# A hybrid retention/SSD block on one core: scaling on GpSimd, decay exponentials with a bias, tile places, order at the end

## The chip, the cores and the metric

One program on one core of a Trainium2 chip. The metric is the device time of one execution in microseconds (us); the kernel before took 846.1 us (median of three runs, 846.07 to 846.16).

## The reference

One layer of a streaming encoder over 512 frames, with 16 learned meta tokens ahead of them, width 1024, all in float32:

```python
hn = rmsnorm(h, norm1_w);  proj = hn @ w_in           # 7184 columns: q k v g z x B C dt
y_ret = retention(q, k, v, g)                          # 8 heads of 128, block-causal, decayed state
y_ssd = ssd(z, conv(x B C), dt)                        # 16 heads of 64 in 4 groups, state 128
#   lmat = exp(a_cs[l] - a_cs[s]) for l >= s;  y = (C B^T * lmat) @ (x dt) + C @ state + x * d_skip
#   y = y * silu(z);  y = y * rsqrt(mean(y*y) over the group's 256) * norm_w
h = h + concat(y_ret, y_ssd) @ w_out
h = h + relu(rmsnorm(h, norm2_w) @ w_ff1)**2 @ w_ff2
return rmsnorm(h, final_norm_w)                        # meta rows dropped
```

## The kernel before

Every large product is made of three TensorE passes over operands that are split in a high part and a low rest (high x high, high x low, low x high). The split is done on the fly for every weight tile: ACT copies the raw tile into the high half of a tile `wh`, DVE subtracts to get the low half (`split`, L163 to L165). Raw weights come by DMA into four buffers `wr`, split ones live in four buffers `wh`.

The program runs through these stages: the SSD projections, group by group (`ssd_proj`, four groups g: B, C, two halves of x, then z), with the scan of the group before (`ssd_core`) woven into them; the retention heads (q, k, v, g) with their cores; the output product; the first FFN product in Strassen-like sub-products (`product`); the second FFN product; and the last norm. A framework scheduler then sets the order of every engine's instructions by its own estimates of when operands are ready. Each engine works its stream strictly in that order, so an instruction that waits holds all behind it.

**Places.** A split tile starts at a multiple of 256 bytes, and the class `cls` of a unit shifts it by 64 bytes times the class (`wh_tile`). The other operand is the split normalised input `hnh`/`hnl`, read from column 0 (meta tokens and 256 frames: products of 272 columns), from column 16 (all frames), or from column 272 (products of 256 columns), which lie 0, 64 and 64 bytes past a multiple of 256. For q, k, v, g, x, B, C the weights are stationary and the input moves; for z it is the other way round. "Distance" below is stationary start minus moving start, modulo 256 bytes, in steps of 64. Before, the products of 256 columns have distance 0 for x, 1 for B, C and k, 2 for v; z has 1, 0 and 3 in the groups 1, 2 and 3.

**The scan of a group.** `lt` (four heads, 128 x 512 each) is loaded by DMA from a DRAM copy of the running sums (`acsd`, L504). `decay` makes the decay matrix of each head: for each of four chunks DVE adds a per-partition value and takes the minimum with 0 (L509), then ACT takes one Exp of the whole head (L510); later DVE multiplies by the masked C B^T (L574). Products `yo` and `yd` give y, DVE gates it with silu(z) (L593), ACT takes squares with sums (L596), GpSimd makes (mean + eps)^-0.5 (L600, L601), DVE scales the four chunks of y (L603), TensorE transposes y (`ytp`, L610) and ACT writes it out (L611).

**ACT's tables.** Exp and Silu need different tables; a load (ACT_TABLE_LOAD) stands wherever the stream goes from one to the other.

**The end.** For each of four row blocks b, `fin_b` adds the product to the residual on DVE (L1065), squares on ACT (L1067), (sum)^-0.5 on GpSimd (L1073, L1074), and `scale_b` (L1083 to L1086) scales one half on DVE and one on ACT, with a DMA each. `scale_b(b - 1)` is written behind the add of block b.

Of the kernel before, what the change touches and what calls it, by code (L numbers as in the profile page):

```python
# [37 lines left out]
C_Q, C_K, C_V, C_G, C_Z, C_X, C_B, C_C, C_DT = 0, 1024, 2048, 3072, 4096, 5120, 6144, 6656, 7168  # L38
# [37 lines left out]
def kernel(ctx, tc, x, meta, xtr, wzd, nfw, w_in, w_out, w1, w2, hrows, pcols, crope, cmask, cpack, cident, out, gpow):  # L76
    nc = tc.nc
    ACT, DVE, POOL, PE = nc.scalar, nc.vector, nc.gpsimd, nc.tensor
# [9 lines left out]
    whl = ctx.enter_context(tc.tile_pool(name="whl", bufs=4))  # L88
# [7 lines left out]
    xt = [perm.tile([P, D], F32, name=f"xt{b}") for b in range(NB)]  # L96
# [17 lines left out]
    tna = sp.tile([P, NCH, SH], F32, name="tna")  # L114
# [78 lines left out]
    def u_cols(w, c0, c1, cls=(2, 2)):  # L193

        def ld(c, j):
            return (lambda r: r[:, j * 1024:(j + 1) * 1024].rearrange("p (k c) -> p k c", c=P),
                    w[:, c:c + P].rearrange("(k p) c -> p k c", p=P))
        if c1 == c0 + P:
            loads = [(lambda r: r.rearrange("p (k c) -> p k c", c=2 * P),
                      w[:, c0:c0 + 2 * P].rearrange("(k p) c -> p k c", p=P))]  # L200
            views = lambda r, j: r.rearrange("p (k c) -> p k c", c=2 * P)[:, :, j * P:(j + 1) * P]
        else:
            loads = [ld(c0, 0), ld(c1, 1)]
            views = lambda r, j: r[:, j * 1024:(j + 1) * 1024].rearrange("p (k c) -> p k c", c=P)
        return Unit(loads, views, P, cls)

    def u_z(w, c0, cls):

        loads = [(lambda r: r.rearrange("p (k c) -> p k c", c=256),
                  w[:, c0:c0 + 256].rearrange("(k p) c -> p k c", p=P))]  # L210
        return Unit(loads, lambda r, j: r[:, j * 1024:(j + 1) * 1024].rearrange("p (k c) -> p k c", c=256), 256, (cls, cls))

    class UnitZ0(Unit):

# [25 lines left out]
    def add(key, u):  # L240
        U[key] = u
        order.append(u)

    add(("z", 0), UnitZ0())
    for g in range(SG):
        add(("bc", g), u_cols(w_in, C_B + P * g, C_C + P * g))
        add(("x", g), u_cols(w_in, C_X + 256 * g, C_X + 256 * g + P, (1, 1)))
        if g:
            add(("z", g), u_z(w_in, C_Z + 256 * g, (g - 1) % 3))
    for h in range(RH):  # L250
        add(("qk", h), u_cols(w_in, C_Q + P * h, C_K + P * h, (1, 2)))
# [245 lines left out]
    def ssd_core(g, r):  # L497
        bf, cf, xf = r["bf"], r["cf"], (r["x0"], r["x1"])
        hs = slice(4 * g, 4 * g + 4)

        pl = [sw.tile([P, T], F32, tag="lt", name="lt", bufs=4) for _ in range(4)]
# [3 lines left out]
        def decay(h):  # L505
            hh = 4 * g + h
            for c in range(NB):
                v = pl[h][:, c * P:(c + 1) * P]
                DVE.tensor_scalar(v, v, tna[:, c + 1, hh:hh + 1], 0.0, op0=ALU.add, op1=ALU.min)  # L509
            ACT.activation(pl[h], pl[h], AF.Exp)  # L510


        xdt = sw.tile([P, NB, 256], F32, tag="xdt", name="xdt", bufs=1)
# [56 lines left out]
        cbm = sw.tile([P, T], F32, tag="cbm", name="cbm", bufs=1)  # L570
        DVE.tensor_tensor(cbm.rearrange("p (c l) -> p c l", l=P), ps.rearrange("p (c l) -> p c l", l=P),
                          tri.unsqueeze(1).broadcast_to([P, NB, P]), op=ALU.mult)
        for h in range(4):
            DVE.tensor_tensor(pl[h], cbm, pl[h], op=ALU.mult)  # L574
        yield
        y = sw.tile([P, NB, 256], F32, tag="y", name="y", bufs=1)
        ss = small.tile([P, NB], F32, tag="ss4", name="ss4")
        for c2 in range(2):
            po = psum(pm, "yo")
            for cc in range(2):  # L580
                c = 2 * c2 + cc
# [5 lines left out]
            for cc in range(2):  # L587
                c = 2 * c2 + cc
# [5 lines left out]
            for cc in range(2):  # L594
                c = 2 * c2 + cc
# [3 lines left out]
        rs = small.tile([P, NB], F32, tag="rs4", name="rs4")  # L599
        POOL.tensor_scalar(rs, ss, 1.0 / 256, EPS, op0=ALU.mult, op1=ALU.add)  # L600
        POOL.tensor_tensor(rs, rs, powc[:, :NB], op=ALU.pow)  # L601
        for c in range(NB):
            DVE.tensor_scalar(y[:, c, :], y[:, c, :], rs[:, c:c + 1], None, op0=ALU.mult)  # L603
        yield
        if g < SG - 1:
            yield
# [30 lines left out]
    for g in range(SG):  # L637
        r = {} if g else r0
# [106 lines left out]
    for h in range(RH):  # L745
        r = {}
# [106 lines left out]
    def split_hs(q, pool, src):
        t = HS.get(q)
        if t is None:
            t = HS[q] = pool.tile([P, 2, 4, 256], F32R, name=f"hs{q}")
        split(t[:, 0].rearrange("p k n -> p (k n)"), t[:, 1].rearrange("p k n -> p (k n)"), src)

    def tok_gen(b):

        for _ in range(LAG):
            yield
        h = b // 2
        for j in range(2):
            ps = psum(pm, "tp")
            for k in range(4):
                PE.transpose(ps[:, k * P:(k + 1) * P], xt[b][:, (4 * j + k) * P:(4 * j + k + 1) * P], ident)
            dst = R[j][h].rearrange("p (k n) -> p k n", n=256)[:, :, (b % 2) * P:(b % 2 + 1) * P]
            for k in range(4):
                ACT.activation(dst[:, k, :], ps[:, k * P:(k + 1) * P], AF.Copy, scale=pc[:, PC_N2 + 4 * j + k:PC_N2 + 4 * j + k + 1])  # L870
            if b == 1:
                split_hs(1 + j, None, R[j][0])
            yield
        if b < 3:
            return
        sub = lambda o, x, y: DVE.tensor_tensor(o, x, y, op=ALU.subtract)
        t2 = FP["a"][:, 14:16, :].rearrange("p a b -> p (a b)")
        sub(R[0][0], R[0][1], R[0][0])
        sub(t2, R[1][1], R[0][0])
        while "t" not in FP:  # L880
            yield
        split_hs(6, FP["t"], t2)
        yield
        split_hs(5, FP["t"], R[0][0])
        sub(R[0][1], R[1][1], R[0][1])
        yield
        split_hs(7, FP["t"], R[0][1])
        yield
        sub(R[1][0], R[1][0], t2)
        split_hs(4, FP["t"], R[1][0])  # L890
        yield
        split_hs(3, FP["t"], R[1][1])
# [13 lines left out]
    loads = [0, 2, 4, 1, 6, 7] + list(range(8, 2 * NG))  # L906
# [31 lines left out]
    for g in range(NG):  # L938
        p = at[(6, g)]
# [3 lines left out]
    def w1_prep(n, pool=None):  # L943
        if n >= len(seq) or n in wsp:
            return
        q, g = seq[n]
        src = {1: lambda: quarter(g, 0, 0), 2: lambda: quarter(g, 0, 1), 3: lambda: quarter(g, 0, 1), 4: lambda: quarter(g, 1, 1),
               5: lambda: s1s[g], 6: lambda: quarter(g, 0, 0), 7: lambda: quarter(g, 1, 0)}[q]()
        t = wh_tile(pool or whl, 1)
        split(t[:, 0, :], t[:, 1, :], src)  # L950
        wsp[n] = t.rearrange("p y (k c) -> p y k c", c=256)
        if q == 3:
            done.add(2 * g)
        if all(at[(i, g)] in wsp for i in (4, 7)):
            done.add(2 * g + 1)
        next_loads()
# [25 lines left out]
    def product(n):  # L982
# [95 lines left out]
    def scale_b(b):  # L1078
        o = out[b * P:(b + 1) * P, :]
        w = 256 if b == NB - 1 else 512  # L1080
        for c in range(0, 512, w):
            l, r = slice(c, c + w), slice(512 + c, 512 + c + w)
            DVE.scalar_tensor_tensor(yo[b][:, r], xt[b][:, r], rss[b], nwb[:, r], op0=ALU.mult, op1=ALU.mult)  # L1083
            nc.sync.dma_start(out=o[:, r], in_=yo[b][:, r])
            ACT.activation(yo[b][:, l], yo[b][:, l], AF.Copy, scale=rss[b])
            nc.scalar.dma_start(out=o[:, l], in_=yo[b][:, l])  # L1086

    FP["s"].release()
# [10 lines left out]
    nwb = fin.tile([P, D], F32, name="nwb")  # L1099
# [53 lines left out]
```

## Time and profile before

| | |
|---|---|
| median of three runs | 846.1 us |
| the profiled execution | 847.2 us, of it the span 845.4 us |
| PE (matmul) busy | 832.1 us, 98% of the span |
| DVE, ACT, POOL busy | 556.5, 411.2, 29.8 us |
| ACT table loads | 24, 1.28 us each |
| mean granted TensorE clock | 0.998 of 2.4 GHz |

A busy PE in this profile is an engine with matmuls in flight. They overlap: one of 256 columns is listed with about 0.28 us, but the next one starts 0.11 to 0.12 us after it. So rates are read from starts, not from durations.

### The profile page before, as it was taken

What the parts mean: (1) busy time and instruction counts of PE and PEld (TensorE: products, weight loads), DVE (VectorE), ACT (ScalarE), POOL (GpSimd) and SP (SyncE); (2) the same over time, 40 slices, a digit from 0 to 9 for tenths busy, and PEclk for the clock granted to TensorE, in tenths of its full rate; (3) what the DMA queues carried; (4) which work ended last, traced back from release to release, by engine and by line L of the source; (5) the groups of instructions that cost most, each with busy time, mean ns of one, the idle gap of its engine ahead of it and who ended that gap; (6) DMA issues with size and microseconds to landing.
All of it is one profiled execution on the core that took longest, in us unless ns stands there. A gap on an engine that the chain in (4) does not pass through costs nothing.

```text
span 845.4 us, 13366 instructions
## 1 busy us (share of the span) xinstructions
PE 832.1 (98%) x5556; PEld 759.2 (90%) x5556; DVE 556.5 (66%) x874; ACT 411.2 (49%) x693; POOL 29.8 (4%) x62
## 2 busy tenths in 40 slices
PE   8999999999999999999999999999999999999996
PEld 7999999999889999999888889999999888888884
DVE  6788997968745554556365539988887554474442
ACT  7755737272422233232453548577667643354432
POOL 1000000010000000000000000000000000010001
PEclk9999999999999999999999999999999999999999
DMA  9751333332331313131213213333334523332002
GB/s 316 252 178 50 100 101 100 95 106 76 101 100 50 100 51 100 51 101 50 100 53 102 96 50 100 101 100 101 100 101 137 188 100 99 100 100 100 0 1 100
DMA packets 85373, 84.70 MB, mean 100 GB/s; under 512 B 2464, under 2 KB 67744, under 8 KB 85312
## 3 DMA queue, kind: packets, MB, share of 16 engines
q1 hardware_dynamic: 84016, 81.68, 30.7%
q10 hardware_dynamic: 1296, 2.16, 0.7%
q8 instruction: 43, 0.70, 0.3%
q14 instruction: 18, 0.15, 0.1%
HBM read 81.71 MB, written 2.13 MB: 99 GB/s over the span
## 4 chain that ended last, share of the span: by engine, by line
PE 90%; DVE 3%; ACT 3%; DMA 2%; issue 2%; POOL 0%; POOLq 0%; ACTq 0%; SPq 0%
PE acc L781 10%; PE acc L782 10%; PE acc L780 10%; PE fb L998 7%; PE fd L998 5%; PE fa L998 4%; PE pz L473 3%; PE pj L344 3%; PE pj L342 3%; PE pj L343 3%; PE pv L344 2%; PE pv L343 2%; PE pv L342 2%; PE pk L342 2%; PE pk L344 2%; PE pk L343 2%
## 5 line engine op out<-in xcount | busy, mean ns | idle before, releaser
L164 ACT ACTIVATE wh<-wr 128x1024 fp32r<-128x1024 f32 x146 | 153.8, 1057 | 207.2 <-issue 81.6
L165 DVE TENSOR_TENSOR wh<-wr,wh 128x1024 fp32r<-128x1024 f32 x146 | 177.8, 1219 | 107.4 <-ACT wh L164 107.2
L781 PE MATMUL acc<-wh,mh 128*128 128x512 f32 x370 | 144.1, 390 | 0.5 <-DVE mh L165 0.5
L780 PE MATMUL acc<-wh,mh 128*128 128x512 f32 x370 | 144.2, 391 | 0.0
L782 PE MATMUL acc<-wh,mh 128*128 128x512 f32 x370 | 144.1, 389 | 0.0
L781 PEld LDWEIGHTS acc<-wh,mh 128*128 128x128 f32 x370 | 69.5, 188 | 15.0 <-DVE mh L165 0.9
L782 PEld LDWEIGHTS acc<-wh,mh 128*128 128x128 f32 x370 | 69.5, 188 | 14.6
L780 PEld LDWEIGHTS acc<-wh,mh 128*128 128x128 f32 x370 | 69.4, 188 | 14.0
L342 PE MATMUL pj<-hnh,wh 128*128 128x256 f32 (+2 forms) x256 | 73.7, 288 | 0.0
L343 PE MATMUL pj<-hnl,wh 128*128 128x256 f32 (+2 forms) x256 | 73.2, 286 | 0.0
L344 PE MATMUL pj<-hnh,wh 128*128 128x256 f32 (+2 forms) x256 | 72.5, 283 | 0.0
L998 PE MATMUL fb<-hs,wh 128*128 128x256 f32 x576 | 68.4, 277 | 0.4 <-DVE wh L165 0.4
L998 PEld LDWEIGHTS fb<-hs,wh 128*128 128x128 f32 x576 | 66.8, 188 | 0.7 <-DVE wh L165 0.6
L343 PEld LDWEIGHTS pj<-hnl,wh 128*128 128x128 f32 x256 | 48.5, 189 | 0.1
L342 PEld LDWEIGHTS pj<-hnh,wh 128*128 128x128 f32 x256 | 48.4, 189 | 0.0
L344 PEld LDWEIGHTS pj<-hnh,wh 128*128 128x128 f32 x256 | 48.4, 189 | 0.0
L998 PE MATMUL fa<-hs,wh 128*128 128x256 f32 x384 | 46.3, 277 | 0.3 <-ACT a_lo L1003 0.3
L998 PE MATMUL fd<-hs,wh 128*128 128x256 f32 x384 | 45.2, 277 | 0.0
L998 PEld LDWEIGHTS fa<-hs,wh 128*128 128x128 f32 x384 | 44.7, 188 | 0.5 <-ACT a_lo L1003 0.5
L998 PEld LDWEIGHTS fd<-hs,wh 128*128 128x128 f32 x384 | 44.5, 188 | 0.1
L164 ACT ACTIVATE mh<-a_lo 128x512 fp32r<-128x512 f32 x48 | 29.3, 621 | 19.2 <-PE acc L782 17.1
L165 DVE TENSOR_TENSOR mh<-a_lo,mh 128x512 fp32r<-128x512 f32 x48 | 32.5, 687 | 7.7 <-ACT mh L164 7.6
(270 smaller groups left out, 1646.6 us busy)
## 6 DMA issues: line engine op xcount, KB each, us to landing
wr<-in_w_ff_dram SPq DMA_DIRECT2D x30, 1024.0 KB, 5.3
wr<-in_w_in_dram SPq DMA_DIRECT2D x40, 512.0 KB, 4.8
wr<-in_w_out_dram SPq DMA_DIRECT2D x8, 1024.0 KB, 5.0
wr<-in_w_in_dram SPq DMA_DIRECT2D x7, 1024.0 KB, 8.1
lt<-acsd SPq DMA_DIRECT2D x16, 256.0 KB, 4.2
xt<-in_x_dram SPq DMA_DIRECT2D x4, 512.0 KB, 6.8
a_lo<-in_w_ff_dram SPq DMA_DIRECT2D x2, 1024.0 KB, 6.4
wzr<-in_wzd_dram ACTq DMA_DIRECT2D x4, 272.0 KB, 6.1
```

Source lines behind the costliest of these rows:

```text
L164: ACT.activation(dst_h, src, AF.Copy)
L165: DVE.tensor_tensor(dst_l, src, dst_h.bitcast(F32), op=ALU.subtract)
L342: PE.matmul(ps[:, :n], lhsT=wh[:, k, :], rhs=hnh[:, k, t0:t0 + n], start=(k == 0), stop=False)
L343: PE.matmul(ps[:, :n], lhsT=wh[:, k, :], rhs=hnl[:, k, t0:t0 + n], start=False, stop=False)
L344: PE.matmul(ps[:, :n], lhsT=wl[:, k, :], rhs=hnh[:, k, t0:t0 + n], start=False, stop=(k == KT - 1))
L473: PE.matmul(o, lhsT=a[:, k, tk], rhs=zp[k // 4][y][:, k % 4, :], start=(i == 0), stop=(i == len(seq) - 1))
L780: PE.matmul(acc[b], lhsT=s[:, 0, tk], rhs=wh[:, kk, :], start=(k == 0), stop=False)
L781: PE.matmul(acc[b], lhsT=s[:, 1, tk], rhs=wh[:, kk, :], start=False, stop=False)
L782: PE.matmul(acc[b], lhsT=s[:, 0, tk], rhs=wl[:, kk, :], start=False, stop=(k == nk - 1))
L998: PE.matmul(o, lhsT=w[:, y, k, cs], rhs=h[:, z, k, :], start=(q in (1, 6, 5) and t == 0 and k == 0 and i == 0), stop=(k == 3 and i == 2), ...
```

## The change

- `decay`: the 64 DVE instructions (add, minimum) and 16 Exps of 128 x 512 become 64 Exps of 128 x 128 on ACT that take the added value as their bias; the minimum moves into the multiply by C B^T, now min with 1 and multiply (a scalar_tensor_tensor on DVE, 16 of them).
- The four scalings of y of each group go from DVE to GpSimd, behind its power.
- Classes: x from 1 to 2, z from 0, 1, 2 to 0, v from 3 to 2. The distances of all products of 256 columns become 1; those of 272 columns become 2 for x (were 1) and 2 for v (were 3). In the first FFN product `wh` goes from class 1 to 2 and the input tiles `hs` move by 64 bytes as well, so that the distance stays 1; their pool is now filled in one place.
- In `scale_b` the DVE and the ACT scaling are pinned behind what is written before them on their engine.

```diff
-    def u_z(w, c0, cls):
+    def u_z(w, c0):
...
-        return Unit(loads, lambda r, j: r[:, j * 1024:(j + 1) * 1024].rearrange("p (k c) -> p k c", c=256), 256, (cls, cls))
+        return Unit(loads, lambda r, j: r[:, j * 1024:(j + 1) * 1024].rearrange("p (k c) -> p k c", c=256), 256)
...
-        add(("x", g), u_cols(w_in, C_X + 256 * g, C_X + 256 * g + P, (1, 1)))
+        add(("x", g), u_cols(w_in, C_X + 256 * g, C_X + 256 * g + P))
...
-            add(("z", g), u_z(w_in, C_Z + 256 * g, (g - 1) % 3))
+            add(("z", g), u_z(w_in, C_Z + 256 * g))
...
-        add(("vg", h), u_cols(w_in, C_V + P * h, C_G + P * h, (3, 1)))
+        add(("vg", h), u_cols(w_in, C_V + P * h, C_G + P * h, (2, 1)))
...
-                DVE.tensor_scalar(v, v, tna[:, c + 1, hh:hh + 1], 0.0, op0=ALU.add, op1=ALU.min)
-            ACT.activation(pl[h], pl[h], AF.Exp)
+                ACT.activation(v, v, AF.Exp, bias=tna[:, c + 1, hh:hh + 1])
...
-            DVE.tensor_tensor(pl[h], cbm, pl[h], op=ALU.mult)
+            DVE.scalar_tensor_tensor(pl[h], pl[h], 1.0, cbm, op0=ALU.min, op1=ALU.mult)
...
-            DVE.tensor_scalar(y[:, c, :], y[:, c, :], rs[:, c:c + 1], None, op0=ALU.mult)
+            POOL.tensor_scalar(y[:, c, :], y[:, c, :], rs[:, c:c + 1], None, op0=ALU.mult)
...
+    hs12.tile([P, 16], F32, name="pad3")
     HS = {q: hs12.tile([P, 2, 4, 256], F32R, name=f"hs{q}") for q in (1, 2)}
...
-        t = wh_tile(pool or whl, 1)
+        t = wh_tile(pool or whl, 2)
...
+                FP["t"].tile([P, 16], F32, name="pad5")
+                HS.update({q: FP["t"].tile([P, 2, 4, 256], F32R, name=f"hs{q}") for q in (6, 5, 7, 4, 3)})
...
-            DVE.scalar_tensor_tensor(yo[b][:, r], xt[b][:, r], rss[b], nwb[:, r], op0=ALU.mult, op1=ALU.mult)
+            tc.keep_in_program_order(
+                DVE.scalar_tensor_tensor(yo[b][:, r], xt[b][:, r], rss[b], nwb[:, r], op0=ALU.mult, op1=ALU.mult))
             nc.sync.dma_start(out=o[:, r], in_=yo[b][:, r])
-            ACT.activation(yo[b][:, l], yo[b][:, l], AF.Copy, scale=rss[b])
+            tc.keep_in_program_order(ACT.activation(yo[b][:, l], yo[b][:, l], AF.Copy, scale=rss[b]))
```

What this does to the streams is shown at three places. The first is ACT while the scan of group 0 starts (`xf` is the second half of x after its convolution, which TensorE transposes next; `btm` a transposed piece of B, `hq` the first state). Before:

```order
L527 ACTIVATE bt_685<-btp_692 128x384
L164 ACTIVATE wh_907<-wr_822 128x1024
L427 ACT_TABLE_LOAD
L427 ACTIVATE xf_672<-acc_667,pc_84 128x528
L510 ACT_TABLE_LOAD
L510 ACTIVATE lt_674<-lt_674 128x512
L523 ACTIVATE btm_109<-mtp_686 16x128
L510 ACTIVATE lt_675<-lt_675 128x512
L164 ACTIVATE wh_998<-wr_996 128x1024
L559 ACTIVATE hq_803<-st0_797 128x256
```

The same place now:

```order
L526 ACTIVATE bt_685<-btp_692 128x384
L164 ACTIVATE wh_903<-wr_818 128x1024
L509 ACTIVATE lt_674<-lt_674,tna_101 128x128 x2
L427 ACT_TABLE_LOAD
L427 ACTIVATE xf_672<-acc_667,pc_84 128x528
L509 ACT_TABLE_LOAD
L509 ACTIVATE lt_674<-lt_674,tna_101 128x128
L522 ACTIVATE btm_109<-mtp_686 16x128
L509 ACTIVATE lt_674<-lt_674,tna_101 128x128
L509 ACTIVATE lt_675<-lt_675,tna_101 128x128 x4
L509 ACTIVATE lt_676<-lt_676,tna_101 128x128 x4
L509 ACTIVATE lt_677<-lt_677,tna_101 128x128 x4
```

Two Exps of the first head stand ahead of the Silu of `xf`; twelve more and one of the first head stand between `btm` and `hq`.

The second place is the second half of group 1's scan, where y is squared (`xdd`), on ACT; `lt_1701` or `lt_1693` is the first head of group 2. Before:

```order
L427 ACTIVATE cf_1399<-acc_1394,pc_84 128x512
L596 ACTIVATE xdd_1197,ss4_1402<-y_1401 128x256 x2
L164 ACTIVATE wh_1582<-wr_1579 128x1024
L596 ACTIVATE xdd_1197,ss4_1402<-y_1401 128x256 x2
L427 ACTIVATE xf_1483<-acc_1478,pc_84 128x528
```

Now:

```order
L595 ACTIVATE xdd_1193,ss4_1394<-y_1393 128x256 x2
L427 ACTIVATE cf_1391<-acc_1386,pc_84 128x512
L164 ACTIVATE wh_1574<-wr_1571 128x1024
L509 ACT_TABLE_LOAD
L509 ACTIVATE lt_1693<-lt_1693,tna_101 128x128
L427 ACT_TABLE_LOAD
L427 ACTIVATE xf_1475<-acc_1470,pc_84 128x528
L595 ACTIVATE xdd_1193,ss4_1394<-y_1393 128x256 x2
```

The second pair of squares now stands behind an Exp of the next group, two table loads and a Silu. On DVE at the same place, from the gating of y on, before:

```order
L593 TENSOR_TENSOR y_1401<-y_1401,zs_1135 128x512
L425 SCALAR_TENSOR_TENSOR acc_1478<-pre_1424,pc_84,acc_1478 128x528
L404 MEMSET pre_1515 128x3
L407 TENSOR_TENSOR pre_1515<-pj_1517,rsr_113 128x272
L165 TENSOR_TENSOR wh_1576<-wr_1510,wh_1576 128x1024
L603 TENSOR_SCALAR y_1401<-y_1401,rs4_1503 128x256 x4
```

Now:

```order
L592 TENSOR_TENSOR y_1393<-y_1393,zs_1131 128x512
L404 MEMSET pre_1507 128x3
L407 TENSOR_TENSOR pre_1507<-pj_1509,rsr_113 128x272
L165 TENSOR_TENSOR wh_1568<-wr_1502,wh_1568 128x1024
L407 TENSOR_TENSOR pre_1507<-pj_1535,rsr_113 128x256
L165 TENSOR_TENSOR wh_1574<-wr_1571,wh_1574 128x1024
L423 TENSOR_SCALAR acc_1561<-pre_1507,pc_84 128x528
L404 MEMSET pre_1735 128x3
L425 SCALAR_TENSOR_TENSOR acc_1561<-pre_1507,pc_84,acc_1561 128x528 x2
L165 TENSOR_TENSOR wh_1732<-wr_1571,wh_1732 128x1024
L425 SCALAR_TENSOR_TENSOR acc_1561<-pre_1507,pc_84,acc_1561 128x528
```

DVE no longer stops for the scaling of y; it runs on through splits and convolution adds while GpSimd scales.

The third place is the end of DVE's stream. Before:

```order
L1065 SCALAR_TENSOR_TENSOR xt0_78<-acc_7408,rs20_4693,xt0_78 128x512
L1083 SCALAR_TENSOR_TENSOR yo0_6894<-xt0_78,rss0_6902,nwb_6885 128x512
L1065 SCALAR_TENSOR_TENSOR xt1_79<-acc_7409,rs21_4694,xt1_79 128x512
L1083 SCALAR_TENSOR_TENSOR yo1_6895<-xt1_79,rss1_6903,nwb_6885 128x512
L1065 SCALAR_TENSOR_TENSOR xt2_80<-acc_7410,rs22_4695,xt2_80 128x512
L1083 SCALAR_TENSOR_TENSOR yo2_6896<-xt2_80,rss2_6904,nwb_6885 128x512
L1065 SCALAR_TENSOR_TENSOR xt3_81<-acc_7411,rs23_4696,xt3_81 128x256 x2
```

Now:

```order
L1067 SCALAR_TENSOR_TENSOR xt0_78<-acc_7396,rs20_4679,xt0_78 128x512
L1067 SCALAR_TENSOR_TENSOR xt1_79<-acc_7397,rs21_4680,xt1_79 128x512
L1086 SCALAR_TENSOR_TENSOR yo0_6882<-xt0_78,rss0_6890,nwb_6873 128x512
L1067 SCALAR_TENSOR_TENSOR xt2_80<-acc_7398,rs22_4681,xt2_80 128x512
L1086 SCALAR_TENSOR_TENSOR yo1_6883<-xt1_79,rss1_6891,nwb_6873 128x512
L1067 SCALAR_TENSOR_TENSOR xt3_81<-acc_7399,rs23_4682,xt3_81 128x256 x2
L1086 SCALAR_TENSOR_TENSOR yo2_6884<-xt2_80,rss2_6892,nwb_6873 128x512
```

The add of each block now stands ahead of the scaling of the block before. ACT's squares and scalings change places in the same way, and its last two scalings alternate with their two DMA issues, where both scalings stood first before.

## Rows read from the trace of the kernel before

**Rows 1.** Page, busy time of the engines (share of the span) xinstructions.
```profile
PE 832.1 (98%) x5556; PEld 759.2 (90%) x5556; DVE 556.5 (66%) x874; ACT 411.2 (49%) x693; POOL 29.8 (4%) x62
```
**Rows 2.** Timeline of PE: start us, us, engine, line, output<-inputs; products for x and z.
```profile
121.14 0.37 PE L342 MATMUL pj<-hnh,wh 128*128 128x272 f32 x1
...
124.19 0.28 PE L342 MATMUL pj<-hnh,wh 128*128 128x256 f32 x1
...
127.06 0.28 PE L473 MATMUL pz<-wh,hnh 128*128 128x256 f32 x1
...
129.94 0.71 PE L610 MATMUL ytp<-idt,y 128*128 128x128 f32 x5
...
172.67 0.28 PE L473 MATMUL pz<-wh,hnh 128*128 128x256 f32 x1
...
175.50 0.71 PE L610 MATMUL ytp<-idt,y 128*128 128x128 f32 x5
```
**Rows 3.** Timeline of PE, one head's products for k and v.
```profile
225.01 0.37 PE L342 MATMUL pk<-hnh,wh 128*128 128x272 f32 x1
...
228.13 0.28 PE L342 MATMUL pk<-hnh,wh 128*128 128x256 f32 x1
...
230.87 0.38 PE L711 MATMUL kv<-mk 128*128 128x128 f32 x2
...
235.69 0.28 PE L342 MATMUL pv<-hnh,wh 128*128 128x256 f32 x1
...
238.57 0.38 PE L727 MATMUL o<-vt,pt 128*128 128x128 f32 x2
```
**Rows 4.** Timeline of ACT at group 0's scan; [idle before <- what ended it].
```profile
52.09 0.74 ACT L427 ACTIVATE xf<-acc,pc 128x528 f32<-128x528 f32 x1 [2.06 <-DVE acc L425]
53.91 1.28 ACT L510 ACT_TABLE_LOAD   x1 [1.08 <-DMA lt<-acsd]
```
**Rows 5.** Timeline of PE at the same place.
```profile
54.62 0.27 PE L519 MATMUL mtp<-idt,xf 128*16 128x128 f32 x1
...
57.42 0.67 PE L553 MATMUL st<-xmw,btm 128*128 128x256 f32 x2 [0.69 <-ACT btm L523]
```
**Rows 6.** Groups by line and form, ACT: xcount | busy us, mean ns | idle before.
```profile
L510 ACT ACT_TABLE_LOAD x9 | 11.5, 1283 | 1.2 <-DMA lt<-acsd 1.1
...
L708 ACT ACTIVATE vt<-vtp,rsc 128x128 f32<-128x128 f32 x32 | 9.0, 369 | 0.0
```
**Rows 7.** Tile lt, 108 to 125 us: loads for group 2, time to landing.
```profile
L503 SPq DMA_DIRECT2D lt<-acsd x4: 338/382/386, 120.7 to 122.1; - x4
...
DMA to landing us min/median/max: 3.2/3.5/4.2
```
**Rows 8.** Timeline of PE at group 0's transposes of y.
```profile
84.68 1.13 PE L610 MATMUL ytp<-idt,y 128*128 128x128 f32 x8 [0.55 <-DVE y L603]
```
**Rows 9.** Timeline of ACT, the squares of group 1's second half.
```profile
123.92 0.42 ACT L596 ACTIVATE xdd<-y 128x256 f32<-128x256 f32 x1 [4.04 <-DVE y L593]
```
**Rows 10.** Timeline of POOL, groups 0 and 1.
```profile
82.84 0.20 POOL L600 TENSOR_SCALAR rs<-ss 128x4 f32<-128x4 f32 x1 [57.53 <-ACT xdd L596]
...
124.92 1.20 POOL L600 TENSOR_SCALAR rs<-ss 128x4 f32<-128x4 f32 x1 [40.78 <-ACT xdd L596]
126.20 1.01 POOL L601 TENSOR_TENSOR rs<-rs,powc 128x4 f32<-128x4 f32 x1
```
**Rows 11.** Timeline of DVE, around the second of these.
```profile
124.85 1.22 DVE L165 TENSOR_TENSOR wh<-wr,wh 128x1024 fp32r<-128x1024 f32 x1
```
**Rows 12.** Timeline of DVE at the end.
```profile
837.87 0.75 DVE L1083 SCALAR_TENSOR_TENSOR yo<-xt,rss,nwb 128x512 f32<-128x512 f32 x1 [1.69 <-POOL rss L1074]
838.54 0.87 DVE L1065 SCALAR_TENSOR_TENSOR xt<-acc,rs,xt 128x256 f32<-128x256 f32 x2
```
**Rows 13.** Timeline of PE and of ACT's queue at the end.
```profile
834.37 2.88 PE L807 MATMUL acc<-wh,mh 128*128 128x512 f32 x12
...
841.49 0.84 ACTq L1086 DMA_DIRECT2D out_dram<-yo  x2
```

More of the change, by code (lines that the diff above doesn't have):

```diff
@@ L845 @@
     wx = tc.alloc_tile_pool(name="wx", bufs=3, side="right", reuse_waits="tile")
+    hs12.tile([P, 16], F32, name="pad3")
     HS = {q: hs12.tile([P, 2, 4, 256], F32R, name=f"hs{q}") for q in (1, 2)}
+    hs12.tile([P, 48], F32, name="pad4")
     a_hi = ar.tile([P, 8, T], F32, name="a_hi")
@@ L851, with split_hs @@
     FP = {}
[L853 to L856, printed above, removed]
+    def split_hs(q, src):
+        t = HS[q]
         split(t[:, 0].rearrange("p k n -> p (k n)"), t[:, 1].rearrange("p k n -> p (k n)"), src)
@@ L871, in tok_gen @@
             if b == 1:
-                split_hs(1 + j, None, R[j][0])
+                split_hs(1 + j, R[j][0])
             yield
@@ L881, in tok_gen @@
             yield
-        split_hs(6, FP["t"], t2)
+        split_hs(6, t2)
         yield
-        split_hs(5, FP["t"], R[0][0])
+        split_hs(5, R[0][0])
         sub(R[0][1], R[1][1], R[0][1])
         yield
-        split_hs(7, FP["t"], R[0][1])
+        split_hs(7, R[0][1])
         yield
         sub(R[1][0], R[1][0], t2)
-        split_hs(4, FP["t"], R[1][0])
+        split_hs(4, R[1][0])
         yield
-        split_hs(3, FP["t"], R[1][1])
+        split_hs(3, R[1][1])
     def fin1(b, acc):
@@ L1039, in first_products @@
                 FP["t"] = tc.alloc_tile_pool(name="hst", bufs=1, side="right", reuse_waits="tile")
+                FP["t"].tile([P, 16], F32, name="pad5")
+                HS.update({q: FP["t"].tile([P, 2, 4, 256], F32R, name=f"hs{q}") for q in (6, 5, 7, 4, 3)})
+                FP["t"].tile([P, 48], F32, name="pad6")
             if n == at[(6, 0)]:
```

## The prediction, made before the changed kernel was run

> **What bounds the kernel now.** I read the busy times first: PE has matmuls in flight for 98% of the span, DVE is busy for 66% and ACT for 49% [rows 1]. So only two things move the end: the pace of PE's own products, and the few places where PE waits. I then read PE's timeline, from starts and not from durations. Twenty-four products of 256 columns for k take 230.87 - 228.13 = 2.74 us, for v 238.57 - 235.69 = 2.88 [rows 3]; for x 127.06 - 124.19 = 2.87, for z 2.88 in group 2 and 2.83 in group 3 [rows 2]. Same shape, same number, other distance of the two tiles. Last came the waits of PE and what ended them: 0.55 us at group 0's transposes of y, ended by DVE's scaling [rows 8], and 0.69 at `st`, ended by ACT's copy of `btm` [rows 5]. The profiled execution took 847.17 us, 845.4 of it the span, about 1.1 above the median. I work out differences against it and take them off or add them to the median, 846.1.
>
> **The places.** Distance 1 is the fastest for 256 columns: 2.74 us for 24, against 2.87 at 0 (x), 2.88 at 2 (v), 2.88 at 0 (z, group 2) and 2.83 at 3 (z, group 3) [rows 2, 3]. All of these go to 1. By blocks of 24: v has eight heads, 8 x 0.14 = 1.12; x two halves in four groups, 8 x 0.13 = 1.04; z four blocks in group 2, 4 x 0.14 = 0.56, and four in group 3, 4 x 0.09 = 0.36. Against it stand the 272-column products of x, which go from distance 1 (124.19 - 121.14 = 3.05) to 2; the k products at another distance than 1 show 228.13 - 225.01 = 3.12 [rows 2, 3], so 8 x 0.07 = 0.56 is lost. For v's 272 columns (3 to 2) no row gives both distances; I take nothing, with the same 0.56 either way as bounds. The first FFN product moves both tiles by 64 bytes and keeps its distance: nothing. Sum -1.12 - 1.04 - 0.56 - 0.36 + 0.56 = **-2.5 us**. These products stand on the bound engine, so the whole of it counts where no wait eats it.
>
> **The end.** The last product ends at 834.37 + 2.88 = 837.25 [rows 13], but the last add starts at 838.54, behind the scaling of block 2 that waited for GpSimd until 837.87 [rows 12]. With the add first, up to 838.54 - 837.29 = 1.25 goes. But ACT now has the scaling of block 2 and a DMA issue behind the squares of block 3, and each scaling of block 3 alternates with its issue, where the two issues stood last together (841.49 and half of 0.84 later [rows 13]). So the late thing next is ACT's last issue. Bounds -1.25 and 0; I take **-0.6**, halfway.
>
> **The exponentials off the path.** ACT gets 64 Exps of 128 x 128. The trace has none; the nearest row is a scaled ACTIVATE of that shape, 369 ns each and 9.0 us for 32, so 0.28 a piece when they overlap [rows 6]. Sixty-four are 18 us, less the 16 large ones. The streams hold 38 table loads where there were 24: 14 x 1.283 = 18.0 us more [rows 6]. DVE loses 64 instructions. ACT was half idle, so all of this is worth nothing by itself: PE's products hide it. It matters only where something PE needs soon stands behind it, which is at group 0's start and before the transposes of y.
>
> The rows have the next ACTIVATE right behind a load: one load and its Exp stand 1.28 apart. The Trainium skill (ScalarE: Activation LUTs, the measured figure under the section on what ACT_TABLE_LOAD costs) adds a drain of about 1380 ns to every switch. By that rule the squares of groups 1 and 2, each with one exposed load ahead, would come about 1.4 later each, and my sum would rise by an estimated 2.8; I follow the rows.
>
> **Group 0's start.** Two Exps now stand ahead of the Silu of `xf`. They need `lt`, and `lt` landed when ACT's wait of 1.08 ended, at 53.91 [rows 4]. Then 0.65 for two Exps, 1.28 for the table, 0.74 for the Silu: 53.9 + 0.65 + 1.28 + 0.74 = 56.6. PE wants `xf` at 54.62 [rows 5]: a wait of 2.0. The wait of 0.69 for `btm` falls away, and DVE, which was also behind here, has less to do; PE may be level again by the first `yd`. Bounds 0.3 and 1.3 (2.0 - 0.7); I take **+0.5**, nearer to the low end because the products after it are waiting for DVE anyway.
>
> **The scaling of y on GpSimd.** This is the large term. I walk each group from Y, the start of PE's next projection right behind the last `yd` (121.14 in group 1 [rows 2]). The loads of the next group's `lt` go out at 120.7 = Y - 0.44 and take 3.2 to 4.2, median 3.5 [rows 7], so they land at Y + 3.1. Now Exps stand ahead of the second pair of squares, and a waiting Exp holds the squares, the Silus and the split copies behind it on ACT.
>
> Group 1: Exp 0.37, table 1.28, Silu 0.74 and two squares of 0.42 [rows 4, 6, 9] give Y + 3.1 + 0.37 + 1.28 + 0.74 + 0.84 = Y + 6.35, where the first of these squares started at 123.92 = Y + 2.78 before [rows 9]. GpSimd's power takes at least 0.20 + 1.01 and some 0.2 of gaps [rows 10]: Y + 7.75. PE is at the transposes at Y + 8.8 (129.94 before [rows 2]). So there is 1.05 for four scalings, of which DVE did one in about 0.28 of its 1.14 in all.
>
> What one scaling costs on GpSimd is the unknown. The same small instruction took 0.20 us when DVE stood idle and 1.20 when it started beside DVE's split [rows 10]; it ended at 126.12, the split at 124.85 + 1.22 = 126.07 [rows 11]. So a GpSimd instruction is held until DVE's instruction with two inputs from SBUF is over. DVE's stream now runs such instructions without a stop while GpSimd scales, since the scaling no longer stands in it. Bounds for one scaling: 0.2 and 1.2. I take 0.8: some 0.3 of its own and half a split's wait.
>
> - Group 1: four at 0.8 are 3.2, so Y + 10.95 against Y + 8.8: wait 2.2.
> - Group 2: two more Exps (0.55) ahead of the squares, Y + 11.5 against Y + 8.7: wait 2.8.
> - Group 0: PE comes early, at Y + 6.2, since only 4 products of z stand ahead (24 x 0.127 + 24 x 0.114 + 4 x 0.114). Six Exps (1.7) and two squares: Y + 5.65; power, Y + 7.1; it needs two pieces soon, 1.6: wait 2.5.
> - Group 3: no Exps follow and DVE has little to do; 0.3.
>
> Sum 7.8, less the old wait of 0.55 [rows 8]: **+7.25**, with +2.2 if a scaling takes 0.3, and some +11 if each takes 1.2.
>
> **Total:** -2.5 - 0.6 + 0.5 + 7.25 = +4.65, so 846.1 + 4.65 = **850.8 us**.
>
> **Rivals.**
>
> 1. *GpSimd scales undisturbed, 0.3 a piece.* Waits 1.4 (group 0), 0.2, 0.9 and 0.2, less 0.55: +2.2, and -2.5 - 0.6 + 0.5 + 2.2 = -0.4: **845.7**. For it: 0.20 us beside an idle DVE [rows 10]. Against it: rows 11, and that the two engines meet in every group. This is also what the Trainium skill says where it compares engines (GPSIMD Engine Reference, on engine selection): elementwise work with one input is roughly at line rate there. Yet its specifications table on the same page names contention with DVE instructions of two SBUF inputs, and with that the trace agrees (1.20 against 0.20).
> 2. *The waits vanish (the other side: faster).* If the squares of group 0 end by Y + 4.2 rather than Y + 5.65 and those of group 2 a microsecond sooner, the scaled y is there when PE comes. That takes loads that land after 3.2 [rows 7], Exps at 0.2 and GpSimd at 0.2 a piece. Then only the places, the end and the old wait count, and group 0's start is level: -2.5 - 0.6 - 0.55 = -3.65: **842.5**. Against it: six Exps of 0.28 behind a landing at Y + 3.1 cannot be over by Y + 4.2 unless the loads are issued earlier.
> 3. *Each scaling waits out a whole split, 1.2 a piece.* +1.6 in groups 1 and 2 and +0.8 in group 0 on top of the forecast: 850.8 + 4.0 = **854.8**. For it: the one overlap that I can read ended exactly with the split. Against it: many of DVE's instructions there are shorter than a split.
>
> **How the numbers follow.** Forecast 0.50, rival 1 0.28, rival 2 0.12, rival 3 0.10. About 0.2%, 1.7 us, is what a measurement can tell from no change: 844.4 to 847.8. Faster: all of rival 2 and a third of rival 1 (the tail's 0.6 more, group 0's start at its low end), 0.22. Same: the rest of rival 1 and 0.05 of the forecast's low end (a scaling at 0.5), 0.23. Slower: 0.55. The range goes from 843.2, short of rival 2, to 855.5, past rival 3's value; the forecast's own range is 848 to 853.5.
>
> **What would show it.** Right: PE shows waits of 2 to 3 us at `ytp` in groups 0, 1 and 2, ended by POOL's y; single scalings on POOL near 0.8, their ends on the ends of DVE's splits and convolution adds; 24 products of 256 columns in 2.74 everywhere; a wait of about 2 at `mtp` for `xf` near 54.6; the last add starting near the end of the last product. Wrong: scalings of 0.3 and PE's waits at `ytp` under 1.5 (rival 1); squares that end well before Y + 5 (rival 2); 256-column products of x, v or z still at 2.87 (the places do not do it); or an end that comes no earlier against the last product.

## The result and the profile after

The changed kernel took 868.9 us (median of 4 runs, 867.45 to 869.64) against 846.1 (846.00 to 846.16): ratio 1.026, interval 1.024 to 1.028. It is slower, as forecast, but by 22.8 us where I had forecast 4.7, and the time lies far outside my range. The profiled execution took 867.45 us, 865.7 of it the span, 20.3 more than before. (Before, the profiled execution lay 1.1 above its median, now it lies 1.4 below, so the traces show 20.3 of the 22.8.)

I first lined the two timelines up by the starts of the same products on PE:

| product on PE | before | after | after - before |
|---|---|---|---|
| first `yo`, group 0 | 63.55 | 63.62 | +0.07 |
| first `yo`, group 1 | 110.07 | 115.84 | +5.77 |
| first `yo` of the second half, group 2 | 164.19 | 174.67 | +10.48 |
| the same, group 3 | 209.48 | 225.77 | +16.29 |
| first `o`, head 0 | 238.57 | 260.80 | +22.23 |
| first output product | 412.05 | 433.30 | +21.25 |
| last twelve products | 834.37 | 855.82 | +21.45 |
| end of the span | 845.4 | 865.7 | +20.3 |

So 4.7 to 5.9 us are lost in each of four stretches, which hold the transposes of y of groups 0, 1, 2 and 3. After them the heads give back 1.0 and the end 1.15. PE's busy time is hardly longer than before [rows 1]; the page's line of busy times:

```profile
PE 837.2 (97%) x5556; PEld 763.1 (88%) x5556; DVE 541.3 (63%) x794; ACT 439.9 (51%) x755; POOL 49.3 (6%) x78
```

The waits of PE (line, what it waited for: us in total, times, longest) name the place:

```profile
PE ytp L609 <- POOL y L602: 15.8, 15, 3.4
PE mtp L518 <- ACT xf L427: 1.3, 1, 1.3
```

The first was 0.55, once, for DVE [rows 8]. The timeline of PE shows it from the side of the transposes, in groups 0 and 2:

```profile
84.53 0.44 PE L609 MATMUL ytp<-idt,y 128*128 128x128 f32 x2 [3.45 <-POOL y L602]
86.21 0.47 PE L609 MATMUL ytp<-idt,y 128*128 128x128 f32 x1 [1.25 <-POOL y L602]
...
188.57 0.48 PE L609 MATMUL ytp<-idt,y 128*128 128x128 f32 x1 [2.50 <-POOL y L602]
189.47 0.48 PE L609 MATMUL ytp<-idt,y 128*128 128x128 f32 x1 [0.42 <-POOL y L602]
190.37 0.48 PE L609 MATMUL ytp<-idt,y 128*128 128x128 f32 x1 [0.42 <-POOL y L602]
```

In group 2 a piece arrives every 0.90 us. POOL's timeline has four scalings, one behind the other, in all four groups. They take 1.05 to 1.66 us on the mean of a group; taken one by one they run from 0.92 to 2.46:

```profile
83.47 6.63 POOL L602 TENSOR_SCALAR y<-y,rs 128x256 f32<-128x256 f32 x4
...
135.83 5.16 POOL L602 TENSOR_SCALAR y<-y,rs 128x256 f32<-128x256 f32 x4
...
187.00 4.21 POOL L602 TENSOR_SCALAR y<-y,rs 128x256 f32<-128x256 f32 x4
...
233.68 4.48 POOL L602 TENSOR_SCALAR y<-y,rs 128x256 f32<-128x256 f32 x4
```

What I had not looked for at all stands in the table by stretches (start:end, length, PE busy and count, granted TensorE clock, DMA share, GB/s):

```profile
80.00:104.00 24.00, 18.50 (x141) 0.93 0.29 89
130.00:150.00 20.00, 16.17 (x123) 0.91 0.44 129
180.00:200.00 20.00, 16.23 (x116) 0.83 0.54 159
226.00:246.00 20.00, 17.20 (x74) 0.83 0.58 177
```

Before, these stages ran at 1.00. By slices of 1 us the clock goes from 1.00 (2.4 GHz) to 0.50 (1.2 GHz) in each of the four groups once PE has waited at the transposes, and comes back after PE has worked on without a wait. Group 0 now, and below it the slice before that holds the old wait:

```profile
85.00:86.00 1.00, 0.00 (x0) 1.00 1.15 346
86.00:87.00 1.00, 0.79 (x4) 0.57 0.99 300
87.00:88.00 1.00, 1.00 (x7) 0.50 0.01 2
88.00:89.00 1.00, 1.00 (x6) 0.50 0.41 50
89.00:90.00 1.00, 0.46 (x3) 0.73 0.90 294
90.00:91.00 1.00, 0.85 (x7) 1.00 1.06 377
```

```profile
84.00:85.00 1.00, 0.45 (x5) 1.00 0.00 0
```

Added up over the slices (1 less the granted clock, times the slice), 1.70, 1.71, 3.41 and 3.41 us of full clock are missing, 10.2 in all. About 1.5 of that falls into the waits themselves, so waits and clock are not quite a sum.

In groups 0 to 2 the chain of this loss begins on ACT. Group 1's squares there, once at 123.92 [rows 9], now:

```profile
129.65 1.28 ACT L509 ACT_TABLE_LOAD   x1 [4.09 <-DMA lt<-acsd]
130.95 0.40 ACT L509 ACTIVATE lt<-lt,tna 128x128 f32<-128x128 f32 x1
131.37 1.28 ACT L427 ACT_TABLE_LOAD   x1
132.67 0.74 ACT L427 ACTIVATE xf<-acc,pc 128x528 f32<-128x528 f32 x1
133.31 0.40 ACT L595 ACTIVATE xdd<-y 128x256 f32<-128x256 f32 x1
```

It is the table load for the Exp that waits for `lt`, not the Exp: the load itself, 1.28 us, comes after the landing.

The other parts did about what I had said. Twenty-four products of 272 and 256 columns of x take 129.95 - 126.82 = 3.13 and 132.67 - 129.95 = 2.72 us [rows 2: 3.05 and 2.87]:

```profile
126.82 0.38 PE L342 MATMUL pj<-hnh,wh 128*128 128x272 f32 x1
...
129.95 0.28 PE L342 MATMUL pj<-hnh,wh 128*128 128x256 f32 x1
...
132.67 0.28 PE L473 MATMUL pz<-wh,hnh 128*128 128x256 f32 x1
```

And the last add starts where the last product ends (855.82 + 2.88 = 858.70), no longer behind a scaling [rows 12, 13]:

```profile
858.74 0.88 DVE L1067 SCALAR_TENSOR_TENSOR xt<-acc,rs,xt 128x256 f32<-128x256 f32 x2 [1.31 <-PE acc L806]
859.53 0.74 DVE L1086 SCALAR_TENSOR_TENSOR yo<-xt,rss,nwb 128x512 f32<-128x512 f32 x1
```

From the last product's end to the span's end it is 7.0 us, where it was 845.4 - 837.25 = 8.15.

### The profile page after: what moved, and what is told of

Read it like the earlier page. It is cut to its first block, busy times and chain, and to the rows that moved or that the text cites. A ratio compares the mean times of both kernels' runs of the same rounds, so it can differ in the third digit from the quotient of the medians.

```text
span 865.7 us, 13376 instructions
## 1 busy us (share of the span) xinstructions
PE 837.2 (97%) x5556; PEld 763.1 (88%) x5556; DVE 541.3 (63%) x794; ACT 439.9 (51%) x755; POOL 49.3 (6%) x78
## 4 chain that ended last, share of the span: by engine, by line
PE 86%; DVE 4%; DMA 3%; POOL 3%; ACT 2%; issue 1%; ACTq 0%; POOLq 0%; SPq 0%; DVEq 0%
PE acc L779 10%; PE acc L781 10%; PE acc L780 10%; PE fb L997 7%; PE fd L997 5%; PE fa L997 4%; PE pz L473 3%; PE pj L344 3%; PE pj L342 3%; PE pj L343 3%; POOL y L602 2%; PE pq L342 2%; PE pq L344 2%; PE pq L343 2%; PE pv L344 2%; DMA lt<-acsd 2%
## 5 line engine op out<-in xcount | busy, mean ns | idle before, releaser
L164 ACT ACTIVATE mh<-a_lo 128x512 fp32r<-128x512 f32 x48 | 29.3, 621 | 22.8 <-PE acc L781 17.2
L473 PE MATMUL pz<-wh,hnh 128*128 128x256 f32 x192 | 39.2, 301 | 0.1
```

Of the source, the lines that this page charges most:

```text
L473: PE.matmul(o, lhsT=a[:, k, tk], rhs=zp[k // 4][y][:, k % 4, :], start=(i == 0), stop=(i == len(seq) - 1))
```

## The experiments

I set theory A (the scaling itself, by GpSimd's own time, and then the clock) against theory B (the Exps make y late; where the scaling stands matters little). Times are medians; a part of the runs with the first FFN product's old tiles is some 3 to 6 us longer (ffn_old, below), which widens the intervals of the ratios and pulls some away from the medians.

| kernel | us | ratio, interval | PE waits at `ytp`, us | clock missing, us |
|---|---|---|---|---|
| before, in four series | 845.9 to 846.5 | | 0.6 | 0 |
| the change | 868.9 | 1.026 (1.024 to 1.028) | 15.8 | 10.2 |
| pool_only | 859.6 | 1.013 (1.010 to 1.017) | 10.1 | 5.1 |
| after_dve | 846.0 | 0.998 (0.997 to 1.000) | 2.8 | 0 |
| exp_only | 849.0 | 1.003 (1.000 to 1.005) | 2.9 | 0 |
| no_exp_pool | 858.3 | 1.013 (1.010 to 1.017) | 9.9 | 5.1 |
| warm | 860.2 | 1.016 (1.013 to 1.020) | 0.9 | 0 |
| after_tt | 861.5 | 1.020 (1.017 to 1.023) | 11.5 | 8.5 |
| after_act | 846.9 | 1.001 (1.000 to 1.002) | 4.3 | 1.7 |
| no_exp_dve | 843.6 | 0.995 (0.992 to 0.997) | 0.5 | 0 |
| places_tail_act | 844.0 | 0.998 (0.996 to 1.000) | 0.4 | 0 |
| ffn_old | 845.7 | 0.998 (0.996 to 1.001) | 0.4 | 0 |

The kernels ran in three series, each beside the kernel before: pool_only, after_dve, exp_only and no_exp_dve; then no_exp_pool, warm, pieces and ffn_old; then after_tt, after_act and places_tail_act. "Clock missing" leaves out the last microseconds of a run, when PE has nothing left to do.

**pool_only**: the kernel before with one line changed.

```diff
-            DVE.tensor_scalar(y[:, c, :], y[:, c, :], rs[:, c:c + 1], None, op0=ALU.mult)
+            POOL.tensor_scalar(y[:, c, :], y[:, c, :], rs[:, c:c + 1], None, op0=ALU.mult)
```

> The kernel before with one change: the four scalings of y of each group go to GpSimd. Theory A (the scaling itself costs the time: 0.9 us a piece on GpSimd even with an idle DVE, and TensorE's granted clock then falls to 0.50 for some microseconds after PE has waited): the squares are not delayed here, so the waits are shorter than with the whole change, 1 to 4 us a group, and where a wait is long the clock falls again: 852 to 860. Theory B (the Exps and table loads ahead of the squares are what makes y late; the place of the scaling matters little): 846 to 849, with PE's waits at the transposes under 1 us a group.

Measured 859.6, as theory A has it, with no Exp moved. Theory B falls as the main cause.

**after_dve**: the changed kernel with that line put back.

```diff
-            POOL.tensor_scalar(y[:, c, :], y[:, c, :], rs[:, c:c + 1], None, op0=ALU.mult)
+            DVE.tensor_scalar(y[:, c, :], y[:, c, :], rs[:, c:c + 1], None, op0=ALU.mult)
```

> The changed kernel with only the scalings of y back on DVE; Exps, places and end as changed. Theory A: the four waits of 15.8 us in all and the stretches of granted clock 0.50 go; what stays is about 1 us at the start of group 0 and up to 1 us a group where the squares are late; with -1.15 at the end and -2.5 from the places 842.5 to 846. Theory B: y is still late by the Exps, 852 or more, waits of over 2 us at the transposes, now ended by DVE.

846.0, at the upper end of what A allowed: beside the Exps, that one line is worth 868.9 - 846.0 = 22.9 us, the whole difference. The waits left are the Exps':

```profile
PE ytp L609 <- DVE y L602: 2.8, 3, 1.1
...
PE mtp L518 <- ACT xf L427: 1.1, 1, 1.1
```

**exp_only**: the kernel before with the change of `decay` and of the multiply alone.

```diff
-                DVE.tensor_scalar(v, v, tna[:, c + 1, hh:hh + 1], 0.0, op0=ALU.add, op1=ALU.min)
-            ACT.activation(pl[h], pl[h], AF.Exp)
+                ACT.activation(v, v, AF.Exp, bias=tna[:, c + 1, hh:hh + 1])
...
-            DVE.tensor_tensor(pl[h], cbm, pl[h], op=ALU.mult)
+            DVE.scalar_tensor_tensor(pl[h], pl[h], 1.0, cbm, op0=ALU.min, op1=ALU.mult)
```

> The kernel before with only the decay exponentials changed (64 Exps with bias on ACT, min in the multiply). Theory A: PE gains nothing and loses 0 to 3 us (1.3 for xf in group 0, level again by the first yo; up to 1 us at the transposes of groups 0 and 2): 846 to 849. Theory B: 852 or more.

849.0: alone, the Exps cost 2 to 3 us and gain nothing.

**no_exp_pool**: the changed kernel with that edit undone, so GpSimd scales and the squares are early.

> The changed kernel with the decay as before (adds on DVE, 16 large Exps), scaling on GpSimd, places and end as changed. If the parts only add up: 846.2 + 13.4 (scaling alone) - 2.7 (places and end alone) = 857. If the Exps do nothing to the scaling's cost: 868.9 - 2.4 = 866. Theory A (the late squares and the slow scaling add on the same path, so the Exps cost 9 to 12 here against 2 to 3 where DVE scales): 855 to 859.

858.3. The Exps cost 868.9 - 858.3 = 10.6 us where GpSimd scales and 846.0 - 843.6 = 2.4 where DVE does (against no_exp_dve). Late squares and a slow scaling lie on one path: the time in hand that hides the one is used up by the other. The sum of the other parts (857) is nearly met too, so those two do add; it has nothing for the Exps, and it is their cost that grows beside the other.

**warm**: matmuls of no use in the place of PE's waits.

```diff
             ps = psum(pm, "ytp")
+            if j == 0:
+                for _ in range((24, 16, 16, 12)[g]):
+                    PE.matmul(ps, lhsT=hnh[:, 0, :P], rhs=hnh[:, 0, M:M + T], start=True, stop=True)
```

> The changed kernel with 24, 16, 16 and 12 extra matmuls of 512 columns (0.227 us each at full clock, 15.4 us in all, results overwritten) put on PE ahead of the transposes of y in the four groups, about as much work as PE waited there (15.8 us). Theory A1 (besides the waits, about 10 us go to TensorE's granted clock of 0.50 behind each wait): the waits turn into matmuls, the granted clock stays at 1.00 through all four groups, and the time falls although PE has more to do: 857 to 861. Theory A2 (the low clock costs little, since PE waits for GpSimd there anyway): 866 to 870.

860.2: with 15.4 us of extra work PE is 8.7 us faster. Its table by the same four stretches:

```profile
80.00:104.00 24.00, 23.24 (x174) 1.00 0.29 88
130.00:150.00 20.00, 19.66 (x153) 1.00 0.28 81
180.00:200.00 20.00, 19.34 (x142) 1.00 0.41 121
226.00:246.00 20.00, 19.15 (x115) 1.00 0.31 96
```

So the clock is a cost by itself, by estimate about 9 us of the 22.8: warm gives back 8.7, and the slices outside PE's waits hold as much (10.2 - 1.5). The order of the transposes moves a little too in this kernel, so I give no closer number.

When the clock falls is not settled by the waits alone. In pool_only the waits of group 2 (0.31, 0.57 and 0.76 us) left it at 1.00 and those of group 3 (0.57, 0.57 and 1.09) brought it to 0.50; in no_exp_pool nearly the same waits (0.31, 0.57, 0.77 and 0.57, 0.57, 1.09) did it the other way round.

**pieces**: the four scalings of a group in four forms, by turns (by the number 1.0, that quarter of y stays unscaled). One run, 865.2 us, taken for the durations alone.

```diff
-            POOL.tensor_scalar(y[:, c, :], y[:, c, :], rs[:, c:c + 1], None, op0=ALU.mult)
+            f = (c + g) % 4
+            if f == 0:
+                POOL.tensor_scalar(y[:, c, :], y[:, c, :], rs[:, c:c + 1], None, op0=ALU.mult)
+            elif f == 1:
+                for j in range(2):
+                    v = y[:, c, j * P:(j + 1) * P]
+                    POOL.tensor_scalar(v, v, rs[:, c:c + 1], None, op0=ALU.mult)
+            elif f == 2:
+                POOL.tensor_tensor(y[:, c, :], y[:, c, :], rs[:, c:c + 1].broadcast_to([P, 256]), op=ALU.mult)
+            else:
+                POOL.tensor_scalar(y[:, c, :], y[:, c, :], 1.0, None, op0=ALU.mult)
```

> The changed kernel with the four scalings of y of each group on GpSimd in four forms, by turns: as it is (128x256, factor by row), two halves of 128x128, a tensor_tensor with the factor broadcast, and a multiplication by the number 1.0 (so a quarter of y is not scaled). Theory P1 (the cost is GpSimd's own work per element): beside an idle DVE 0.9 us for 128x256, about 0.45 for a half, no less for the number 1.0. Theory P2 (a fixed cost of the instruction or of its factor by row): a half costs 0.7 to 0.9, or the number 1.0 costs half. Theory P3 (my prediction's: mainly held by DVE): 0.3 to 0.4 beside an idle DVE in each form.

POOL in group 1, then DVE there:

```profile
137.68 0.61 POOL L608 TENSOR_SCALAR y<-y,rs 128x128 f32<-128x128 f32 x1
138.27 0.80 POOL L608 TENSOR_SCALAR y<-y,rs 128x128 f32<-128x128 f32 x1
139.05 0.61 POOL L610 TENSOR_TENSOR y<-y,rs 128x256 f32<-128x256 f32 x1
139.64 0.92 POOL L604 TENSOR_SCALAR y<-y,rs 128x256 f32<-128x256 f32 x1
```

```profile
137.73 0.87 DVE L425 SCALAR_TENSOR_TENSOR acc<-pre,pc,acc 128x528 f32<-128x528 f32 x1
149.43 0.41 DVE L520 TENSOR_TENSOR xmw<-mtp,tdw 16x256 f32<-16x256 f32 x1 [10.83 <-PE mtp L519]
```

DVE is idle from 138.60 on, and the scaling still takes 0.92. In group 0 the number 1.0 takes 0.88 beside an idle DVE, so the factor by row is not it:

```profile
81.62 0.88 POOL L612 TENSOR_SCALAR y<-y 128x256 f32<-128x256 f32 x1
...
83.65 2.38 POOL L604 TENSOR_SCALAR y<-y,rs 128x256 f32<-128x256 f32 x1
```

P3, my prediction's, falls: own time 0.9, not 0.3. Neither P1's half (0.45) nor P2's (0.7 to 0.9) is met. The first half takes 0.61 here, and 0.60 in the groups 2 and 3; the second, 0.80, began beside DVE's add (137.73 + 0.87 = 138.60) and ended 0.47 after it: I count it as held. By estimate 2 x 0.60 - 0.92 = 0.28 is fixed for each instruction and 0.64 goes by its 256 columns, so it is mostly GpSimd's own work by columns, which is nearer to P1. The wait for DVE exists as well: 2.38 for the same form beside DVE's splits. Over the changed kernel's sixteen scalings the mean was (6.63 + 5.16 + 4.21 + 4.48) / 16 = 1.28, so 0.92 own and 0.36 held. One of them, beside a split in group 3 of the changed kernel, first POOL, then DVE:

```profile
235.49 1.77 POOL L602 TENSOR_SCALAR y<-y,rs 128x256 f32<-128x256 f32 x1
```

```profile
235.25 1.23 DVE L165 TENSOR_TENSOR wh<-wr,wh 128x1024 fp32r<-128x1024 f32 x1 [0.45 <-ACT wh L164]
```

**after_tt**: the same engine, but the quicker form.

```diff
-            POOL.tensor_scalar(y[:, c, :], y[:, c, :], rs[:, c:c + 1], None, op0=ALU.mult)
+            POOL.tensor_tensor(y[:, c, :], y[:, c, :], rs[:, c:c + 1].broadcast_to([P, 256]), op=ALU.mult)
```

> The changed kernel with the scaling on GpSimd as a tensor_tensor (the factor broadcast along the row) in place of the tensor_scalar; the same engine, the same places in the streams. In the experiment with four forms such a piece took 0.61 us beside an idle DVE, a tensor_scalar 0.93. Theory P1/P2 (GpSimd's own time a piece is what makes y late): four pieces are 1.3 us shorter a group, the waits fall from 15.8 to 9 to 12 and some low clock goes: 860 to 865. Theory P3 (DVE's instructions hold GpSimd, its own time matters little; a tensor_tensor is held as long): 867 to 870.

861.5, 7.4 less, with the waits at 11.5 and not 15.8: a shorter piece on the same engine gives back a third of the loss, so GpSimd's own time is a cause of the wait.

**after_act**: the same line as an `ACT.activation` with `AF.Copy` and `scale=rs[:, c:c + 1]`.

> The changed kernel with the scaling on ACT (a copy with the factor as scale; an ACTIVATE of 128x256 with a scale takes 0.4 to 0.5 us here). If GpSimd is the cause and not that the scaling left DVE: 845 to 849, a little over the 846.0 with DVE, since ACT has Exps, table loads and split copies in the same microseconds. If any place but DVE is bad: 855 or more.

846.9, 0.9 more than with DVE. So it is GpSimd, not that the scaling left DVE.

**no_exp_dve**: places and end as changed, Exps and scaling as before.

> The kernel before with the places and the order at the end changed, nothing else (Exps and scaling as before). Both theories: 24 products of 256 columns take 2.74 us for x, v and z, -2.5 in all, and the end comes 1.15 sooner after the last product: 842.4 (841.8 to 843.2). If the places are worth nothing: 845.

843.6, by the medians 2.5 to 2.7 less than before, and 0.4 above the top of the range that I expected: places and end give less than the 3.65 behind it. Its trace has 0.9 between the first `yo` of group 0 and head 0 (174.1 us for 175.0), 1.0 in the heads and 0.7 at the end. This is the fastest of all, and it beats both kernels.

**places_tail_act**: the same, with the scaling on ACT.

> A try for a version that beats both: places and end as changed, decay as before, scaling on ACT, which is half idle. The version with the scaling on DVE took 843.6 and waits 0.5 us at the transposes of group 0. If ACT is free there: 843.0 to 843.6. If the scaling stands behind a split copy or a table load on ACT: 844 to 847.

844.0: nothing gained; the wait at the transposes of group 0 was 0.4 against 0.5, and a wait of 1.3 for ACT's silu of z came instead.

**ffn_old**: no_exp_dve with the first FFN product's tiles 64 bytes lower.

```diff
-    hs12.tile([P, 16], F32, name="pad3")
...
-        t = wh_tile(pool or whl, 2)
+        t = wh_tile(pool or whl, 1)
...
-                FP["t"].tile([P, 16], F32, name="pad5")
```

> The places and the end as changed, but the first FFN product's tiles (its weights and its inputs) 64 bytes lower, as before. Theory C (with these places the pace of the 1344 products of 256 columns differs from run to run, 113 or 117 ns, worth 4.7 us): most runs 843.2 to 844.5, some about 848; with the changed places no run was above 844.5. Theory D (the longer runs of the kernel before have another cause): no run above 845, median 843.6.

Six of 12 runs took 843.5 to 844.0, six 847.4 to 849.2. In the kernels that do not scale on GpSimd, 26 of 93 runs with the old tiles, the kernel before among them, were some 3 to 6 us longer than the rest, and 2 of 42 with the new. The profile of exp_only caught one, and its first FFN product shows the pace: seventy products, then the same of the kernel before, which has the same tiles.

```profile
532.39 8.51 PE L997 MATMUL fb<-hs,wh 128*128 128x256 f32 x70 [0.44 <-DVE wh L165]
```

```profile
531.47 8.22 PE L998 MATMUL fb<-hs,wh 128*128 128x256 f32 x70 [0.44 <-DVE wh L165]
```

In the first series it was 13 of 37 with the old tiles against none of 20 with the new, in the third 2 of 23 against 2 of 22. So it is likely, but not shown, that the new tiles make the longer pace rarer; they do not make it impossible. What decides it in a run stays open.

## Why the prediction was wrong

- **The step that failed** is "I take 0.8: some 0.3 of its own and half a split's wait". Its own time is 0.9 (pieces). No row stood behind the 0.3: the nearest were an instruction of 4 columns (0.20) and DVE's time (0.28), neither of which says what 256 columns cost on GpSimd. My upper bound of 1.2 was no bound either: the mean was 1.28, in group 0 1.66, and a single one took 2.46. So PE waited 5.4, 3.8, 3.8 and 2.8 us in the groups 0 to 3, where I had 2.5, 2.2, 2.8 and 0.3. With the own time I would have seen that group 3 waits as well: DVE did its four in 1.15, GpSimd took 4.48 with DVE half idle, and PE lost 5.9 there.
- **The clock was no term of my sum.** All my waits counted once. The runs showed 15.8 us of waits and another 10.2 us of full clock missing; warm gives back 8.7 of it. The trace of before could not show its size, since PE never waited so long there.
- **The Exp's table load** I took to be done before `lt` lands. [Rows 4] showed the opposite: there ACT_TABLE_LOAD itself had waited for `lt`. The squares in group 1 ended at 134.21, 7.39 after 126.82, and not 6.35; in group 0 they ended 6.8 after PE's next projection began, and not 5.65.
- **The sign and the place were right**: PE waits at `ytp` for POOL's y, behind squares made late by Exps; but where I forecast 7.25 there were 15.25 of added waits and 10.2 of clock.
- **The contention** of [rows 10, 11] is real and was over-rated: 0.36 a piece, where I had 0.5. It carries a little over a quarter of a piece's time, not most of it. The rule itself held: the scalings that began beside one of DVE's splits, at 84.46, 187.00 and 235.49, ended 0.80, 0.79 and 0.79 after the split's end, and those that met an idle DVE, such as the one at 140.07, took 0.92.
- **Group 0's start**, +0.5, was +0.07 by the first `yo`, but that small number is chance: the trace of before was itself slow there. From the first `mtp` (near 46) to the first `yo` it took 16.9 us and five other traces with the old Exps 15.6 to 16.5, and the seven with the new ones 16.5 to 17.3. On the mean that is 0.9 more, inside my bounds, though PE waited 1.3 for `xf`, not 2.0.
- **The places** were right in rate: x at 2.72 for 2.74, its 272 columns at 3.13 for 3.12, v gave 0.98 from head 0's `o` to the output product, 0.14 for each of seven heads, as reckoned. In no_exp_dve places and end together gave 2.5 to 2.7 by the medians against 3.1 in my sum. That the first FFN product gets "nothing" holds for the usual run; whether the new tiles spare it the longer one is open.
- **The end**, -0.6, was -1.15, inside my bounds: ACT's last issue does not come later than before. In the traces of no_exp_pool, no_exp_dve, places_tail_act and ffn_old, which have the same end, it was -0.4 to -0.7.
- **Rivals 1 and 2** (845.7 and 842.5) were further off than the forecast. Rival 1's 0.3 a piece was 0.92, and the squares of group 0, which rival 2 wanted by Y + 4.2, ended at Y + 6.8 (81.4 - 74.6). The rule of the Trainium skill (GPSIMD Engine Reference, engine selection) that work with one input is roughly at line rate on GpSimd does not fit this trace: 0.92 us for 128x256 with one input, 0.61 with two. Rival 3 had the right size of a scaling (1.2), by the wrong cause, and was still 14 us short, since it had neither the own time in group 3 nor the clock.
- **The sum again**, by the trace: 15.25 of added waits and 8.7 of clock outside them, less about 1.4 that the places gain by my rates up to head 0, make 22.6 us; between the first `yo` of group 0 and head 0 the two timelines part by 22.23 - 0.07 = 22.2.

## What to carry to other kernels

Before work is moved to another engine, find that engine's own time for that very form and size; a small instruction of the same engine is no bound for a large one. Where TensorE is the bound engine, be ready to price its waits twice: the wait, and the stretch at half the granted clock that may follow. It followed in all four groups of the changed kernel, in two of four in pool_only and no_exp_pool, and in none of after_dve, whose longest wait there was 1.1. And two delays on one path draw on the same time in hand: the Exps cost 2.4 us beside DVE's scaling and 10.6 beside GpSimd's.

## What the runs showed of the hardware

- On GpSimd a multiply of 128x256 by a factor takes 0.92 us as a tensor_scalar and 0.61 as a tensor_tensor with a broadcast factor, with DVE idle.
- A scaling of 128x256 on GpSimd that begins beside one of DVE's splits (1.22 us) is held: three of them ended 0.79 to 0.80 us after the split's end.
- A table load on ACT waits with the instruction it is for: [4.09 <-DMA lt<-acsd] stands at the load.
- Of the same products on the same tiles, the first FFN product's pace differs from run to run (8.51 us for 70 products in exp_only, 8.22 in the kernel before).
- Nearly the same waits of PE left the granted clock at 1.00 in one run and brought it to 0.50 in another (group 2 of pool_only and of no_exp_pool).
